# A two-block transformer kernel on one core: paired score adds, a row-wise output projection, a smaller candidate gather, and twelve hidden tiles computed earlier

## The chip, the cores and the metric

The kernel runs on one core of one Trainium2 chip. The metric is the device time of one execution in microseconds. Before the change three runs took 3618.88, 3621.45 and 3625.93 us; their median is 3621.45 us. The profile used here comes from one further execution of 3620.09 us, of which the traced span is 3618.3 us; the 1.8 us outside the span are left as they are.

## The reference, cut to what matters

Two transformer blocks follow one another on 512 tokens of width 1024, in float32. The first block (attention and a mixture of 32 experts) is not touched. The second block is:

```python
def second_block(x, ...):
    h = rmsnorm(x, norm1_g)
    a_val, a_gate, q, k, v, f_logit, g_a, g_b = jnp.split(h @ w_in, idx, axis=-1)
    ya = conformer_conv(a_val, a_gate, conv_w, ...)            # 31 taps, 1024 channels
    c = jnp.cumsum(log_sigmoid(f_logit + fox_bf), axis=1)
    ob = forgetting_attention(q, k, v, c)                      # 16 heads of 64; s = q k / 8 + c_q - c_k, causal
    yb = ob @ w_fox_out
    x = x + (sigmoid(g_a) * ya + sigmoid(g_b) * yb) @ w_out    # the "last projection"
    x = x + peer_ffn(rmsnorm(x, norm2_g), ...)
    return rmsnorm(x, normf_g)

def peer_ffn(h, ...):                                          # 8 heads, 16384 experts
    s1, s2 = ...                                               # two sets of 128 scores per token and head
    v1, i1 = lax.top_k(s1, 16); v2, i2 = lax.top_k(s2, 16)
    cand = v1[..., :, None] + v2[..., None, :]                 # 256 sums, top 16 of them
    sc, pos = lax.top_k(cand, 16)
    experts = i1[pos // 16] * 128 + i2[pos % 16]
    gates = softmax(sc)
    a = gelu(u[experts] . h) * gates                           # u, v: 16384 x 1024
    return sum(a * v[experts])
```

## The kernel before, in words

A float32 product is made of three matmuls on rounded high and low parts (`mm3`: high by high, high by low, low by high). The splits into parts are made on ScalarE (high part, a copy) and VectorE or GpSimd (low part, a subtraction). The instruction order on each engine is the program's order, written by hand; no scheduler moves anything. Engines meet through buffers and semaphores.

The stages that the change touches, in order of time:

*Attention of block 2* (`attend`, called by `block2`, 32 units: 8 head pairs by 4 query blocks of 128 tokens, keys 128 to 512). In step t the loop issues the scores of unit t, its row maximum and exponential (`soft`), the normalisation of unit t-1, the transposes of unit t-2 and the product with the values of unit t-3. Between the steps it issues six taps of the convolution on VectorE (`background`) and one or two pieces of other projection work (`work`). `scores` computes the two heads of a pair, each from 64 partitions, into two PSUM tiles; behind each one stands a bf16 matmul over 96 partitions that adds the decay c_q - c_k, with weights `L` that `make` builds on VectorE, one instruction per head.

*Last projection* (`block2`, lines 1675 to 1692). For each of 8 blocks of 128 output columns, `zT` multiplies a weight block (stationary) with the 512 tokens (moving), so the result comes out transposed. ScalarE copies it out, four TensorE transposes turn it, VectorE adds it to the rows `xt`, and ScalarE makes four sums of squares.

*Routing* (`peer_route`). For each of 8 heads: two projections, scores, the top 16 of both score sets (`top16`), then `choose` (50 candidate sums, top 16 of them), `ranks` (one-hot of 16 positions by 50), `codes` (times the codes, on GpSimd), `gather` (a reduction over 50). VectorE carries most of it.

*Hidden tiles* (`split_u`, `first`, `first_one`). There are 128 tiles of 128 experts; one `first` is 24 matmuls of 384 columns (tokens 0 to 383; the last 128 tokens take the sparse way) and a GELU into an `act` tile. `NPRE` = 34 of them are issued ahead of the last stage: 20 in routing, 10 in the gate stage, 4 at the start of the last stage.

*Gate stage* (`peer_gates`). In 48 steps of 8 tokens, one-hot tiles `o1`, `o2` are built on GpSimd (three instructions a step), VectorE and ScalarE, multiplied on TensorE (`gps`), and written to DRAM. A `first` is put between the steps, with its low-part split on GpSimd.

*Last stage* (`peer`). 128 iterations. While hidden tiles are left, an iteration holds one `first` and one `second` (18 matmuls of 512 columns); afterwards only a `second`. VectorE also works through 256 gathered rows (`row`) for the last 128 tokens, spread over the iterations.

## Time and profile before

| | us |
|---|---|
| median of three runs | 3621.45 |
| profiled execution, whole | 3620.09 |
| its span | 3618.3 |
| TensorE busy | 3469.0 (96%) |
| VectorE busy | 2951.5 (82%) |
| ScalarE busy | 2029.2 (56%) |
| GpSimd busy | 1189.7 (33%) |

A busy TensorE is not by itself a bound, since matmuls are pipelined and overlap in the records; a stage is read by what the next instruction waited for. Up to 1709 us nothing is changed. The stages that follow are told apart by the lines of their first instructions: attention of block 2 from 1718 us, its gates and two projections from 2046 us, the last projection from 2220 us, routing from 2275 us, the gate stage from 2503 us, the last stage from 2652 us, its part without hidden tiles from 3455 us, the final norm from 3604 us.

### The profile page before, as it was taken

How to read it: one execution, taken by the hardware profiler on the slowest of the kernel's cores; microseconds unless marked ns; L12 is line 12 of the kernel's file. 1: busy time of each engine (PE TensorE's matmuls, PEld its weight loads, DVE VectorE, ACT ScalarE, POOL GpSimd, SP SyncE). 2: the span in 40 equal slices, each digit the busy share in tenths (PEclk: the TensorE clock that was granted, in tenths of full speed). 3: DMA queues.
4: the chain of work that ended last, by engine and by line, in shares of the span. 5: the costliest groups of instructions: out<-in, count | busy, mean ns of one | idle time of the engine just before them, and what ended most of it. 6: DMA issues, size and time to landing. Idle time of an engine off the chain costs nothing.

```text
span 3618.3 us, 48096 instructions
## 1 busy us (share of the span) xinstructions
PE 3469.0 (96%) x16965; PEld 2799.1 (77%) x16966; DVE 2951.5 (82%) x4755; ACT 2029.2 (56%) x3225; POOL 1189.7 (33%) x756
## 2 busy tenths in 40 slices
PE   8899879999999999998999999998999999999998
PEld 5665667777777777776777778787888889988976
DVE  5676489999999999997888754799967777777777
ACT  4555468888888888886434353424853333333333
POOL 0567022222222222220000000467954444433333
PEclk9889989999999999999999999999999999999999
DMA  5322579999999999993121222322578888888886
GB/s 201 103 94 97 184 276 373 367 370 373 363 371 364 369 364 374 369 358 102 68 70 59 70 93 87 102 80 88 210 289 300 300 301 297 296 306 292 294 281 225
DMA packets 229994, 866.56 MB, mean 239 GB/s; under 512 B 21890, under 2 KB 73218, under 8 KB 179060
## 3 DMA queue, kind: packets, MB, share of 16 engines
q1 hardware_dynamic: 131680, 641.33, 47.7%
q0 software_dynamic: 47008, 170.87, 14.5%
q10 hardware_dynamic: 51060, 51.23, 4.2%
q8 instruction: 136, 2.23, 0.2%
q14 instruction: 110, 0.90, 0.1%
HBM read 815.05 MB, written 48.30 MB: 239 GB/s over the span
## 4 chain that ended last, share of the span: by engine, by line
PE 43%; DVE 5%; POOL 3%; ACT 1%; issue 0%; DMA 0%; ACTq 0%; DVEq 0%; POOLq 0%
PE out L2056 15%; PE mm L133 4%; PE mm L134 4%; PE mm L135 4%; PE a L135 4%; PE a L134 4%; PE a L133 4%; POOL o L1954 2%; PE sc L992 1%; DVE eq L1843 1%; POOL ul L1731 1%; PE ot L1046 1%; DVE ex L1851 1%; DVE t L1931 1%; PE pt L1031 0%
## 5 line engine op out<-in xcount | busy, mean ns | idle before, releaser
L1123 DVE TENSOR_TENSOR elo<-raw,ehi 128x1024 fp32r<-128x1024 f32 x384 | 460.6, 1250 | 8.5 <-ACT ehi L1121 8.5
L1121 ACT ACTIVATE ehi<-raw 128x1024 fp32r<-128x1024 f32 x384 | 380.0, 1047 | 9.2 <-PE y L1231 9.2
L135 PE MATMUL a<-hT,ul 128*128 128x384 f32 x1024 | 347.6, 339 | 21.3 <-POOL ul L1731 20.7
L133 PE MATMUL a<-hT,uh 128*128 128x384 f32 x1024 | 347.0, 339 | 1.3 <-ACT uh L1730 1.3
L134 PE MATMUL a<-hT,uh 128*128 128x384 f32 x1024 | 345.3, 337 | 0.0
L1231 PE MATMUL u<-ehi,xgTh 128*128 128x512 f32 x1024 | 337.9, 411 | 0.7 <-ACT xgTh L1165 0.7
L1231 PE MATMUL u<-ehi,xgTl 128*128 128x512 f32 x1024 | 322.9, 396 | 0.0
L1231 PE MATMUL u<-elo,xgTh 128*128 128x512 f32 x1024 | 322.3, 396 | 0.0
L2056 PE MATMUL out<-vh,ah 128*128 128x512 f32 x768 | 302.8, 394 | 1.7 <-ACT ah L125 1.7
L2056 PE MATMUL out<-vl,ah 128*128 128x512 f32 x768 | 303.1, 395 | 0.0
L1123 DVE TENSOR_TENSOR elo<-hT,ehi 128x1024 fp32r<-128x1024 f32 x256 | 296.6, 1218 | 0.5 <-ACT ehi L1121 0.5
L2008 ACT ACTIVATE vh<-vr 128x1024 fp32r<-128x1024 f32 x128 | 135.8, 1061 | 281.9 <-issue 187.4
L2021 POOL DMA_INDIRECT gu<-in_peer_u,pidx x128 | 197.7, 1545 | 248.6 <-DVE gu L2030 225.7
L2021 POOL DMA_INDIRECT gu<-in_peer_v,pidx x128 | 182.5, 1426 | 285.6 <-DVE h L2037 260.0
L2009 DVE TENSOR_TENSOR vl<-vr,vh 128x1024 fp32r<-128x1024 f32 x128 | 156.7, 1225 | 142.6 <-ACT vh L2008 140.3
L1190 POOL DMA_INDIRECT x_d<-ysb,row x31 | 72.0, 2324 | 586.5 <-DVE ysb L1284 527.3
L133 PE MATMUL mm<-hT,sh 128*128 128x512 f32 x648 | 262.8, 406 | 0.0
L135 PE MATMUL mm<-hT,sl 128*128 128x512 f32 x648 | 256.5, 396 | 0.1
L1121 ACT ACTIVATE ehi<-hT 128x1024 fp32r<-128x1024 f32 x256 | 249.2, 1047 | 0.0
L2056 PE MATMUL out<-vh,al 128*128 128x512 f32 x768 | 241.3, 395 | 0.0
L134 PE MATMUL mm<-hT,sh 128*128 128x512 f32 x584 | 231.6, 396 | 0.6 <-DVE hT L1415 0.6
L1231 PEld LDWEIGHTS u<-ehi,xgTl 128*128 128x128 f32 x1024 | 192.9, 188 | 47.0 <-DVE xgTl L1166 0.5
(570 smaller groups left out, 8620.9 us busy)
## 6 DMA issues: line engine op xcount, KB each, us to landing
raw<-in_exp_w SPq DMA_DIRECT2D x192, 1024.0 KB, 7.6
hT<-in_exp_w SPq DMA_DIRECT2D x128, 1024.0 KB, 6.9
sraw<-in_w SPq DMA_DIRECT2D x128, 512.0 KB, 3.3
xt<-in_exp_w SPq DMA_DIRECT2D x64, 1024.0 KB, 8.6
ur<-in_peer_ut SPq DMA_DIRECT2D x128, 512.0 KB, 6.0
vr<-in_peer_vt SPq DMA_DIRECT2D x126, 512.0 KB, 5.7
adaw<-in_ada_w SPq DMA_DIRECT2D x96, 256.0 KB, 4.2
G_d<-G ACTq DMA_DIRECT2D x12, 2048.0 KB, 6.7
```

Source lines behind the costliest of these rows:

```text
L133: nc.tensor.matmul(ps, lh, rh, start=start, stop=False)
L134: nc.tensor.matmul(ps, lh, rl, start=False, stop=False)
L135: nc.tensor.matmul(ps, ll, rh, start=False, stop=stop)
L1121: nc.scalar.activation(hi, src, AF.Copy)
L1123: eng.tensor_tensor(lo, src, hi.bitcast(F), op=OP.subtract)
L1190: nc.gpsimd.indirect_dma_start(out=self.x_d, in_=y, in_offset=None, compute_op=OP.add, out_offset=bass.IndirectOffsetOnAxis(ap=self.row[:, ...
L1231: nc.tensor.matmul(dst[n], x, w[:, n * 512:n * 512 + 512], start=ch >= 8 and k == 0 and x is xh and w is hi, stop=k == KC - 1 and w is lo)
L1954: nc.gpsimd.tensor_scalar(o1[:, i], io, e1[:, t + i:t + i + 1], None, op0=OP.is_equal)
L2008: nc.scalar.activation(hi, r, AF.Copy)
L2009: nc.vector.tensor_tensor(lo, r, hi.bitcast(F), op=OP.subtract)
L2021: nc.gpsimd.indirect_dma_start(out=gu[i], out_offset=None, in_=A["peer_u" if i < 128 else "peer_v"], in_offset=bass.IndirectOffsetOnAxis(a ...
L2056: nc.tensor.matmul(out[tb][n], x, w[:, n * 512:n * 512 + 512], start=i == 0 and x is ah and w is hi, stop=i == 127 and x is al)
```

## The change: what it does

Five edits.

1. *Decay adds in pairs.* The two score matmuls of a unit stand next to each other, then the two decay adds. The decay parts are laid out in 64 partitions per head of a pair instead of 96 shared ones, so that `L` is one tile for both heads and one `make` instruction replaces two.
2. *Last projection by rows.* The tokens are stationary and the weights move in 512 columns; the weights are laid out anew on the host. Four PSUM tiles (token blocks) per half of the columns take 24 matmuls each. There are no copies and no transposes; VectorE adds each tile to `xt`, ScalarE makes one sum of squares for each.
3. *Gather by parts.* 54 candidates instead of 50, in such an order that the first eight of the sixteen winners lie among the first 20. `ranks`, `codes` and `gather` work on 8 by 20 and 8 by 54 elements instead of 16 by 50, with two instructions for each one of before.
4. *Twelve more hidden tiles ahead.* `NPRE` goes from 34 to 46: three more behind the last head of routing, nine more in the gate stage. In the gate stage every second low-part split is issued on VectorE. The additional `act` tiles lie in the buffers of `xt` (and two constants), so the rows `xt` are written to DRAM at the start of routing (four transfers of 512 KB on ScalarE's queue, ahead of the norm gain) and read back in iteration 104 of the last stage.
5. *Order in the last stage.* The product with the gates, then some gathered rows, then the splits, then the rest of the rows, instead of all rows at the end of an iteration; the rows are spread over 128 iterations by the new `NPRE`.

```diff
@@ attend
+            extra = u.get("add")
             for i in range(2):
                 ps = psp.tile([128, 512], F, name=f"sc{i}", bufs=scb)
-                extra = u.get("add")
                 nc.tensor.matmul(ps[:, :n], u["q"][i], u["k"][i], start=True, stop=extra is None)
-                if extra is not None:
-                    nc.tensor.matmul(ps[:, :n], *extra(i), start=False, stop=True)
                 s["ps"].append(ps)
+            if extra is not None:
+                for i in range(2):
+                    nc.tensor.matmul(s["ps"][i][:, :n], *extra(i), start=False, stop=True)
...
@@ block2
-            L[j] = at.tile([96, 2, S], BF, name="L", bufs=2)
-            for i in range(2):
-                h = 2 * j + i
-                nc.vector.tensor_scalar(L[j][:, i], cp, fm[:96, 2 + 2 * h:3 + 2 * h], fm[:96, 3 + 2 * h:4 + 2 * h],
-                                        op0=OP.mult, op1=OP.add)
+            L[j] = at.tile([128, S], BF, name="L", bufs=2)
+            nc.vector.tensor_scalar(L[j], cp, fm[:, 4 + 2 * j:5 + 2 * j], fm[:, 5 + 2 * j:6 + 2 * j],
+                                    op0=OP.mult, op1=OP.add)
...
-                    add=lambda i, j=j, qs=qs, n=n: (L[j][:, i, qs], R[:, :n]),
+                    add=lambda i, j=j, qs=qs, n=n: (L[j][half(i), qs], R[half(i), :n]),
...
-        for j in range(8):
-            ps = out_T(v, sgb)
-            t = pl.tile([128, S], F, name="yT", bufs=2)
-            nc.scalar.activation(t, ps, AF.Copy)
...
+        self.close(psl, psm)
+        pso = self.pool("pso2", bufs=2, space=PSUM)
+        for n in range(2):
+            ps = [pso.tile([128, 512], F, name=f"o{tb}") for tb in range(TB)]
+
+            def part(k, tb, w):
+                ts = slice(tb * 128, tb * 128 + 128)
+                hi, lo = (x.rearrange("p k n -> p (k n)")[:, k % 2 * 512:][:, :512] for x in w)
+                for i, (x, y) in enumerate(((v[k], hi), (v[k], lo), (sgb[k], hi))):
+                    nc.tensor.matmul(ps[tb], x[:, ts], y, start=k + i == 0, stop=k == KC - 1 and i == 2)
+
+            for c in range(4):
+                w = next(self.w2)
+                for k, tb in ([(k, tb) for tb in range(TB) for k in (6, 7)] if c == 3 else
+                              [(k, tb) for k in (2 * c, 2 * c + 1) for tb in range(TB)]):
+                    part(k, tb, w)
+            for tb in range(TB):
+                x = self.xt[tb][:, 512 * n:512 * n + 512]
+                nc.vector.tensor_tensor(x, x, ps[tb], op=OP.add)
+                sq = pl.tile([128, 512], BF, name="sq2", bufs=2)
+                nc.scalar.activation(sq, x, AF.Square, accum_out=self.ss8[:, tb, n:n + 1])
...
-    NPRE, NX = 34, 6
+    NPRE, NX, NH = 46, 6, 12
...
@@ peer_route
+        for tb in range(TB):
+            nc.scalar.dma_start(self.x1_d[tb * 128:tb * 128 + 128, :], self.xt[tb])
         g = nt.tile([128, D], F, name="ngain")
...
-            st[h] = pq.tile([128, TB, 16, 50], F, name="eq"), pos, code
+            st[h] = pq.tile([128, TB, 8, 20 + 54], F, name="eq"), pos, code
...
+        parts = (slice(0, 20), slice(0, 8), 20), (slice(20, 74), slice(8, 16), 54)
...
-            for i in range((1, 2, 2, 2, 2, 2, 2, 3)[h]):
+            for i in range((1, 2, 2, 2, 2, 2, 2, 6)[h]):
...
@@ peer_gates
-                self.split_u(self.done + 1, nc.gpsimd)
+                self.split_u(self.done + 1, (nc.gpsimd, nc.vector)[self.done % 2])
                 self.first()
...
@@ peer
+            a = gated(i + 1) if i < 127 else None
+            rows(i + 0.5)
             self.split_u(self.done + 1, nc.vector)
...
             split(i + 1)
-            nxt = weigh(i + 1) if i < 127 else None
+            nxt = parts(a) if i < 127 else None
             self.first()
             second(i, cur)
...
+            if i == 104:
+                self.x_tiles()
+                for tb in range(TB):
+                    nc.scalar.dma_start(self.xt[tb], self.x1_d[tb * 128:tb * 128 + 128, :])
+            rows(i + 1)
```

Where the order moves. First, TensorE in the attention of block 2, the unit of head pair 4 with 512 keys, before:

```order
L135 MATMUL mm<-hT,sl 128x512
L992 MATMUL sc_16949<-k_16080,q_16072 128x512
L994 LDWEIGHTS L
L994 MATMUL sc_16949<-R,L 128x512
L992 MATMUL sc_16952<-k_16080,q_16072 128x512
L994 LDWEIGHTS L
L994 MATMUL sc_16952<-R,L 128x512
L1031 MATMUL pt_16969<-ident,ap_16797 128x128 x2
```

and after:

```order
L135 MATMUL mm<-hT,sl 128x512
L992 MATMUL sc_16944<-k_16080,q_16072 128x512
L992 MATMUL sc_16946<-k_16080,q_16072 128x512
L996 LDWEIGHTS L
L996 MATMUL sc_16944<-R,L 128x512
L996 LDWEIGHTS L
L996 MATMUL sc_16946<-R,L 128x512
L1032 MATMUL pt_16964<-ident,ap_16792 128x128 x2
```

The second head's scores moved ahead of the first head's decay add, so that two matmuls on 64 partitions each follow one another twice.

Second, ScalarE at the start of routing, with the projection copy `q` and the first hidden tile, before:

```order
L1414 ACTIVATE hT<-tr,colv 128x512 x5
L1730 ACTIVATE uh<-ur 128x1024
L1771 DMA ngain<-in_norm_g 128x1024
L1782 DMA keys<-in_peer_k 128x256 x2
L1796 ACTIVATE q_20826<-mm 128x512
L202 ACTIVATE sh<-sraw 128x1024
```

and after (`x_d<-xt` is the transfer of the rows to DRAM):

```order
L1415 ACTIVATE hT<-tr,colv 128x512 x5
L1732 ACTIVATE uh<-ur 128x1024
L1781 DMA x_d<-xt 128x1024 x4
L1783 DMA ngain<-in_norm_g 128x1024
L1794 DMA keys<-in_peer_k 128x256 x2
L1808 ACTIVATE q_20736<-mm 128x512
L202 ACTIVATE sh<-sraw 128x1024
```

Four transfers now stand ahead of the gain that `h4` on VectorE needs; the copy `q` of the first projection is behind `h4` in its buffer.

Third, VectorE at the start of the gate stage, from the last copy of routing (`pg`) over the first two builds of one-hot tiles (`w`, `o`, `o`), before:

```order
L1918 COPY pg_20672<-g 128x128
L1955 TENSOR_TENSOR w_22933<-io_20674,eT 128x512
L1959 TENSOR_TENSOR o_22931<-io_20674,eT 128x640
L1962 TENSOR_SCALAR o_22932<-io_20674,eT 128x128 x4
L1955 TENSOR_TENSOR w_22950<-io_20674,eT 128x512
L1959 TENSOR_TENSOR o_22948<-io_20674,eT 128x640
L1962 TENSOR_SCALAR o_22949<-io_20674,eT 128x128 x4
L1955 TENSOR_TENSOR w_23011<-io_20674,eT 128x512
```

and after:

```order
L1947 COPY pg_20578<-g 128x128
L1984 TENSOR_TENSOR w_22977<-io_20580,eT 128x512
L1988 TENSOR_TENSOR o_22975<-io_20580,eT 128x640
L1991 TENSOR_SCALAR o_22976<-io_20580,eT 128x128 x4
L1984 TENSOR_TENSOR w_22994<-io_20580,eT 128x512
L1988 TENSOR_TENSOR o_22992<-io_20580,eT 128x640
L1991 TENSOR_SCALAR o_22993<-io_20580,eT 128x128 x4
L1733 TENSOR_TENSOR ul<-ur,uh 128x1024
L1984 TENSOR_TENSOR w_23055<-io_20580,eT 128x512
```

The low-part split `ul` of a hidden tile now stands on VectorE between two builds; the next one follows six builds later, and the splits between them stay on GpSimd.

## Rows read from the trace of the kernel before

**Rows 1.** Windows A:B: length, busy us of PE, PEld, DVE, ACT, POOL; clock, DMA share, GB/s

```profile
1718.00:2046.00 328.00, 327.92 (x1607) 234.42 (x1606) 279.48 (x508) 130.82 (x278) 10.43 (x11) 1.00 0.19 64
2275.40:2503.50 228.10, 203.81 (x1034) 182.47 (x1034) 212.19 (x974) 67.04 (x90) 133.68 (x44) 0.94 0.25 85
2503.50:2652.00 148.50, 137.48 (x1010) 131.68 (x1011) 143.51 (x286) 117.57 (x305) 144.85 (x153) 0.99 0.48 192
2652.00:3455.00 803.00, 801.00 (x4028) 722.50 (x4027) 587.30 (x731) 292.37 (x385) 334.33 (x231) 1.00 0.86 300
3455.00:3604.00 149.00, 147.29 (x629) 117.59 (x628) 120.22 (x141) 57.78 (x75) 51.98 (x32) 1.00 0.77 262
```

**Rows 2.** Timeline of PE, one head pair of block 2: start us, us, instruction

```profile
1883.62 0.48 PE L992 MATMUL sc<-k,q 64*128 64x128 f32 x2
1884.68 0.82 PE L1031 MATMUL pt<-ident,ap 128*128 128x128 f32 x6
...
1916.06 1.12 PE L992 MATMUL sc<-k,q 64*128 64x512 f32 x2
1917.11 0.39 PE L994 MATMUL sc<-R,L 96*128 96x512 bf16 x1
...
1918.71 0.60 PE L1031 MATMUL pt<-ident,ap 128*128 128x128 f32 x4
...
1925.40 0.49 PE L992 MATMUL sc<-k,q 64*128 64x128 f32 x2
```

**Rows 3.** Timeline of PE, a unit of block 1's attention, which has no decay add

```profile
377.96 1.13 PE L992 MATMUL sc<-km,qm 64*128 64x512 f32 x4
```

**Rows 4.** Waits of DVE, 1718 to 2046 (total, times, longest); instruction of `make`

```profile
DVE zc L1508 <- PE mm L135: 16.2, 8, 2.3
DVE aw L1006 <- PE sc L994: 3.6, 4, 2.7
...
L1559 DVE TENSOR_SCALAR L<-cpart,colv x16: 402/403/406, 1717.9 to 1982.4; 96x512 bf16<-96x512 bf16 x16
```

**Rows 5.** Timeline of PE and DVE, first and last of the last projection [idle before]

```profile
2220.12 0.40 PE L133 MATMUL mm<-v,sh 128*128 128x512 f32 x1
...
2270.82 0.66 PE L1683 MATMUL lsum<-ident,yT 128*128 128x128 f32 x4 [2.79 <-ACT yT L1678]
...
2273.76 0.19 DVE L1766 TENSOR_REDUCE ss<-ss 128x4 f32<-128x32 f32 x1 [1.36 <-ACT sq L1689]
```

**Rows 6.** Timeline of DVE and ACT, start of routing

```profile
2290.26 1.49 DVE L1772 SCALAR_TENSOR_TENSOR h<-xt,rs,ngain 128x1024 f32<-128x1024 f32 x1 [2.24 <-DMA ngain<-in_norm_g]
...
2292.71 0.60 ACT L1796 ACTIVATE q<-mm 128x512 f32<-128x512 f32 x1 [4.53 <-DVE h L1772]
```

**Rows 7.** Groups of DVE in routing, six heads: busy us, mean ns, idle before

```profile
L1843 DVE TENSOR_TENSOR eq<-io,pos 128x3200 f32<-128x3200 f32 x6 | 20.9, 3492 | 0.2
L1851 DVE TENSOR_REDUCE ex<-eq 128x64 f32<-128x3200 f32 x6 | 20.8, 3464 | 0.0
```

**Rows 8.** Timeline of PE, end of routing

```profile
2471.82 0.69 PE L135 MATMUL a<-hT,ul 128*128 128x384 f32 x1 [9.98 <-POOL ul L1731]
...
2503.50 1.90 PE L1976 MATMUL gps<-o,o 128*128 128x128 f32 x8 [2.38 <-ACT o L1958]
```

**Rows 9.** Groups in the gate stage; below them a piece of the chain

```profile
L1954 POOL TENSOR_SCALAR o<-io,eT 128x128 f32<-128x128 f32 x142 | 120.1, 866 | 0.0
L1976 PE MATMUL gps<-o,o 128*128 128x128 f32 x752 | 95.5, 282 | 13.4 <-POOL o L1954 10.6 <-ACT o L1958 2.4
...
L1731 POOL TENSOR_TENSOR ul<-ur,uh 128x1024 fp32r<-128x1024 f32 x10 | 26.0, 2598 | 2.3 <-ACT uh L1730 2.2
...
2646.61 5.37 PE gps L1976 x48
```

**Rows 10.** Chain of waits, two iterations of the last stage: start us, us

```profile
2679.76 4.20 PE out L2056 x18
2688.14 4.20 PE out L2056 x18
```

More of the change, by code (lines that the diff above doesn't have):

```diff
@@ L2047, in weigh, with rows @@
             return ah, al
+        def rows(i):
+            nonlocal done
+            k = 128 - self.NPRE
+            while done < min(256, 256 * (min(i, k) + 0.42 * max(0, i - k)) / (k + 0.42 * (127 - k))):
+                row(done)
+                done += 1
+                if done == 253:
+                    g = dn.tile([128, D], F, name="gu", bufs=NG)
+                    nc.sync.dma_start(g, bcast_rows(A["normf_g_2"], D))
+                    gain.append(g)
         def second(i, a):
@@ L2193, in layout @@
         put(n, col(f(n + "_2")))
[L2194 to L2199 removed]
+    par, part, side, p = (a.reshape(128) for a in np.indices((2, 4, 2, 8)))
+    heads, real = 2 * p + par, part < 3
+    put("fox_bf", f("fox_bf_2").reshape(16)[heads].reshape(128, 1))
+    fm = np.zeros((128, 20), np.float32)
+    fm[:, 0], fm[:, 1] = -1.0 * (real & (side == 0)), real & (side == 1)
+    fm[:, 2], fm[:, 3] = -1.0 * (part >= 1), -1.0 * (part >= 2)
+    for j in range(8):
+        fm[:, 4 + 2 * j], fm[:, 5 + 2 * j] = (real & (side == i) & (p == j) for i in (1, 0))
     put("foxmask", fm)
```

132 lines of the change are left out of this document (65 added, 67 removed).

## Prediction

> **What bounds the kernel now.** I read the windows by stage first, then in each changed stage the waits of the engine that ends last, and the timeline where two engines meet. The reader is to see four different limits. In the attention of block 2 TensorE has work all the time (327.9 of 328 us), and VectorE is close behind with 279 us [rows 1]; it waits for TensorE only 16.2 and 3.6 us in all [rows 4]. In routing VectorE works 212 of 228 us while TensorE runs dry in places, ten microseconds at once near the end [rows 1, 8]. In the gate stage GpSimd is busy 144.9 of 148.5 us and never waits between its one-hot builds, while TensorE waits for it [rows 1, 9]. In the last stage TensorE has no gap, and an iteration is a hidden tile of 8.38 - 4.20 = 4.18 us and a `second` of 4.20 us [rows 10]. So work that leaves TensorE counts in full in attention and in the last stage, and work put on TensorE is cheap only where it waits now.
>
> All sums go against the profiled execution, 3620.1 us, which lies 1.4 us under the median of the three runs and inside their spread.
>
> **Decay adds in pairs.** A unit with 512 keys takes 1918.71 - 1916.06 = 2.65 us of TensorE, of which one head's scores take 1917.11 - 1916.06 = 1.05; one with 128 keys takes 1.06 us [rows 2]. The two sizes between lie on a line, so 32 units take 32 x 1.86 = 59 us. Without an add between them, the scores of two heads take 1.13 us together in block 1, as long as one head's here [rows 3]: they overlap, being on different halves of the partitions. The pair saves 1.05 of 2.65, 40%, or 24 us. The bf16 adds come on 64 partitions each now, for which there is no row. If they overlap as well it is half, 30 us; if not, 24 us. VectorE's work stays, except for 8 of 16 `make` instructions of 0.40 us [rows 4]. It can become faster only by the time it waits for TensorE: 16.2 + 3.6 + 3.2 = 23 us, less than TensorE saves. So VectorE becomes the bound here. An engine that works in order does not give back every wait, so I take -20 us, with -14 to -23 for the range.
>
> The Trainium skill says the same on its page "TensorEngine Tiling (Array Packing)", section "PSUM Bottleneck": tiling speeds up TensorE, not the evacuation of PSUM, which can become the limit. By TensorE alone this part would be -27 us and the total 3562 us; by the rule it is VectorE's wait time, as above. No run here shows that limit yet.
>
> **Last projection.** It is 8 x 24 matmuls of 512 columns before and 2 x 96 after, so the matmul time stays: 192 x 4.20/18 = 44.8 us [rows 10], from 2220.12 to 2264.9 [rows 5]. Now TensorE ends at 2270.82 - 2.79 = 2268.0; the transposes between are gone, -3.1 us. From there to the sum of the squares it takes 2273.76 - 2268.0 = 5.7 us (copy, turn, two adds, four squares) [rows 5]; afterwards one add and one square of 512 columns, about 0.75 + 0.6 + 0.2 us from the 1024-column pass and the 512-column copy [rows 6]. That is -4 us. The new PSUM tiles take all banks and may wait for the old ones' last reader, +1 us. I take -6 us (-4 to -7).
>
> **Routing.** One head has 3.49 us of `ranks` and 3.46 us of `gather` [rows 7]; 8 x (20 + 54) elements for 16 x 50 are 0.74 of that, so -0.9 us each. Two instructions for one and 54 candidates for 50 cost some 0.3 us a head (no row; between 0 and 0.6). Seven heads lie ahead of the point where TensorE waits for the split behind `codes` [rows 8]: 7 x 1.5 = -10.5 us (-8 to -12).
>
> At its start four transfers of 512 KB go ahead of the norm gain on ScalarE's queue. VectorE waits 2.24 us for the gain already, and ScalarE's copy of the first projection waits 4.53 us behind `h4` [rows 6]. At the 300 GB/s of the last stage [rows 1] 2.1 MB are 7 us. TensorE's first hidden tile, 4.18 us, stands between projection and scores and covers a part. I take +4 us (0 to +9); without that cover it would be the 9.
>
> At its end there are eight hidden tiles instead of five between the last scores and the gate stage. That stretch takes 2503.50 - 2471.82 = 31.7 us [rows 8], in which TensorE has 20.9 us of tiles; eight are 33.4 us, so it becomes TensorE's. The exponential of the gates stands behind three more GELUs on ScalarE, and `codes` of the last head behind three more splits on GpSimd, so VectorE gets both later. Three tiles cost 12.5 us if nothing hides them; I take +9.5 us (+6 to +12.5).
>
> **Gate stage.** TensorE's own work is 384 products of 5.37/24 = 0.224 us [rows 9], 86 us, and 10 x 4.18 = 42 us of hidden tiles: 128 of 148.5 us. With 19 tiles it is 86 + 79 = 165 us. GpSimd, the bound now with 120 + 26 us [rows 9], loses one split of ten. VectorE gets ten splits, which have no row in this stage: between 1.5 us (the 1024-column pass [rows 6]) and GpSimd's 2.6 us each [rows 9], so 15 to 26 us on top of 143.5 [rows 1]. So TensorE becomes the bound, with VectorE just under it. In order, the GELU holds ScalarE until a tile ends, and the split holds its engine until ScalarE's copy comes, which delays the next build; I put 5 us on that. Together +22 us (+17, TensorE without a gap, to +32).
>
> **Last stage.** Twelve iterations lose their hidden tile: 12 x 4.18 = -50 us. VectorE has 256 gathered rows over fewer long iterations, by the loop's formula 2.54 for 2.38 in each, and was busy 587 of 803 us [rows 1]; that is covered. In the short iterations it is busy 120 of 149 us [rows 1], and the rows rise from 1.00 to 1.07 an iteration: covered, thinly. Reading `xt` back, 2.1 MB where the DMA share is 0.77, may hold up a weight tile: 0 to +4 us; I take 0, since the loads run two tiles ahead.
>
> **Sum.** -20 - 6 - 10.5 + 4 + 9.5 + 22 - 50 = -51 us, so 3569 us. The move of the twelve tiles brings 50 us and gives back 31.
>
> **Rivals.**
> *More is hidden.* The gate stage costs only TensorE's 17 us, the end of routing 6, its start nothing, and attention gives VectorE's whole 23 us: 3620 - 66 = 3554 us. For it speaks that TensorE runs without a gap wherever it is fed now; against it the in-order waits above. Chance 0.16.
>
> *The pairs do not overlap in block 2*, for example because the bf16 adds or the banks' readers keep them apart: attention gives nothing, -31 us, 3589 us. Against it stands what block 1 shows [rows 3]. Chance 0.08.
>
> *The gate stage hides nothing.* VectorE, busy 97% of the stage now, becomes its bound with the splits at their upper price and the blocked builds: nine tiles at full price, +37 us, 3584 us. Chance 0.10.
>
> *Slower: the gathers bound the long iterations.* Each moves two tiles and 2.54 gathered rows of 512 KB and 0.2 MB of gates, 2.6 MB where it was 2.5. The DMA share is 0.86 at 300 GB/s [rows 1], so it should come to 0.89. If the gathers clog the queues, the 81 long iterations stretch; from 9.0 us each (286 GB/s) the 51 us are gone, and at 9.2 us it is 3635 us. It would need the engines to do less than they do now. Chance 0.03.
>
> *The change does not do what it says*: two of the above at once, with no measurable difference. Chance 0.03.
>
> **How the numbers follow.** The forecast has 0.60, around 3569 us. The range from 3552 to 3588 us takes in the bounds of the terms, half of the first rival, the third one and part of the second; outside lie about 0.18. Faster by over 0.2% (about 7 us, what a measurement of this kernel can tell from no change) are the forecast and the first three rivals, 0.94; the same 0.03; slower 0.03.
>
> **What would show it.** In the profile after: score matmuls in groups of four with one duration, the 41.8 us between head pairs [rows 2] down to about 39, and VectorE's wait for `zc` near zero; no transposes in the last projection, and 1.5 to 2 us from its last matmul to the sum of squares; `ranks` and `gather` at 2.6 to 2.7 us in two pieces; the first use of the gain some 7 us later than its issue was; the gate stage 165 to 180 us long, with TensorE busy and GpSimd waiting; 81 iterations of 8.38 us and 47 of 4.20. The prediction is wrong in its main part if attention keeps 41.8 us a pair, if the gate stage grows by more than 32 us, or if a long iteration is over 8.5 us.

## The result and the profile after

Four runs of the changed kernel took 3576.52 to 3579.89 us, median 3578.07 us; four runs of the kernel before beside them 3614.23 to 3625.93, median 3620.16 us. The ratio is 0.9886, with a 95% interval of 0.9872 to 0.9900. The change brings 42 us; the forecast was 51 us, and the time lies inside the range.

The profiled execution took 3579.89 us (span 3578.1), 40.2 us less than the profiled one of before. This is where the 40.2 us are, stage by stage; both columns are starts read from the two traces:

| stretch | before, us | after, us | measured | forecast |
|---|---|---|---|---|
| up to the first score of block 2 (code not changed) | 1720.6 | 1717.8 | -2.8 | 0 |
| first score to first matmul of the last projection | 499.5 | 475.9 | -23.5 | -20 |
| last projection, to the first `nrow` | 55.3 | 47.6 | -7.7 | -6 |
| routing, to the first `gps` | 228.1 | 229.8 | +1.7 | +3 |
| gate stage, first to last `gps` | 148.2 | 182.2 | +34.0 | +22 |
| last `gps` to first `second` | 27.9 | 27.3 | -0.6 | 0 |
| first to last matmul of `second` | 924.4 | 884.0 | -40.4 | -50 |
| tail | 14.3 | 13.4 | -0.9 | 0 |

Two rows miss: the gate stage by 12 us and the last stage by 10 us. The first row is no effect of the change: in the thirteen profiled executions of the changed kernel and its variants that stretch, with the same code, ended between 1717.4 and 1723.8 us. So single profiles are compared here by stretches, not by their ends. How far a stretch varies by itself is seen on the gate stage: in the seven profiles that run it as the change has it, it takes 181.1 to 182.2 us.

**Attention.** The timeline of TensorE (start us, us, instruction), the units with 512 and 128 keys, answers to [rows 2]:

```profile
1899.22 1.13 PE L992 MATMUL sc<-k,q 64*128 64x512 f32 x4
1900.18 0.38 PE L996 MATMUL sc<-R,L 64*128 64x512 bf16 x2
1907.25 0.49 PE L992 MATMUL sc<-k,q 64*128 64x128 f32 x4
1907.58 0.22 PE L996 MATMUL sc<-R,L 64*128 64x128 bf16 x2
...
1946.04 0.49 PE L992 MATMUL sc<-k,q 64*128 64x128 f32 x4
```

Both heads' scores take 1.13 us, exactly block 1's pair [rows 3], and both bf16 adds 0.38 us, what one took before. A unit of 512 keys is down from 2.65 to 1.34 us (1900.18 + 0.38 - 1899.22), and the cycle of a head pair from 41.8 to 1946.04 - 1907.25 = 38.8 us. The waits of VectorE between the first and the last score (total, times, longest), beside [rows 4]:

```profile
DVE k L1564 <- ACT q L1563: 9.2, 7, 1.3
DVE sl L203 <- ACT sh L202: 8.0, 2, 6.3
DVE aw L1007 <- PE sc L996: 2.9, 1, 2.9
DVE zc L1508 <- PE mm L135: 2.6, 7, 0.9
```

The wait for `zc` has gone from 16.2 to 2.6 us. What is left are mainly waits for ScalarE.

**Last projection.** TensorE and VectorE, first matmul, last matmul and sum of squares, beside [rows 5]:

```profile
2193.76 0.47 PE L1683 MATMUL o<-sh,v 128*128 128x512 f32 x1 [0.87 <-DVE v L1665]
...
2237.76 0.40 PE L1683 MATMUL o<-sh,sgb 128*128 128x512 f32 x1
...
2239.74 0.16 DVE L1775 TENSOR_REDUCE ss<-ss 128x4 f32<-128x8 f32 x1 [0.71 <-ACT sq L1694]
```

TensorE runs 2237.76 + 0.40 - 2193.76 = 44.4 us without a gap worth naming, and the squares come 2239.74 - 2238.16 = 1.6 us behind it.

**Start of routing**, beside [rows 6] (the number in brackets is the idle time ahead):

```profile
2256.07 1.23 ACTq L1783 DMA_DIRECT2D ngain<-in_norm_g  x1
...
2263.06 1.28 DVE L1784 SCALAR_TENSOR_TENSOR h<-xt,rs,ngain 128x1024 f32<-128x1024 f32 x1 [8.56 <-DMA ngain<-in_norm_g]
...
2265.29 0.60 ACT L1808 ACTIVATE q<-mm 128x512 f32<-128x512 f32 x1 [10.63 <-PE a L135]
...
2268.35 0.89 DVE L1955 MAX8 v<-s 128x8 f32<-128x128 f32 x4 [4.00 <-PE s L1820]
...
2430.17 0.69 PE L135 MATMUL a<-hT,ul 128*128 128x384 f32 x1 [8.23 <-POOL ul L1733]
```

The gain lands 7.0 us after its issue, behind four writes of 512 KB on the same queue; `h4` waits 8.56 us for 2.24, and ScalarE's `q` 10.63 for 4.53. The first top-16 step starts 27.0 us after `nrow` (2241.37) where it was 24.1: +2.9 us. From there to the point where TensorE waits for the split behind `codes` (the last line, beside [rows 8]) it is 161.8 us where it was 172.3, -10.5 us, and from that point to the first `gps` 41.0 us where it was 31.7, +9.35 us.

**Gate and last stage.** Windows over routing, the gate stage (length, busy us of PE, PEld, DVE, ACT, POOL, granted clock, DMA share, GB/s), beside the second and third of [rows 1]:

```profile
2241.40:2471.20 229.80, 211.70 (x1106) 189.91 (x1106) 204.32 (x1001) 71.00 (x96) 141.04 (x55) 0.97 0.31 101
2471.20:2653.70 182.50, 175.32 (x1226) 170.35 (x1227) 149.30 (x296) 131.28 (x324) 143.73 (x152) 0.98 0.48 182
```

VectorE's busy time in routing falls from 212.2 to 204.3 us. In the gate stage TensorE works 175 of 182.5 us, at a mean granted clock of 0.98. GpSimd is busy 143.7 us; these are the longest waits of the stage, of all engines (total, times, longest):

```profile
POOL ul L1733 <- ACT uh L1732: 33.2, 9, 5.7
DVE ul L1733 <- ACT uh L1732: 30.1, 10, 4.4
ACT xt L1762 <- PE a L135: 19.4, 10, 2.5
ACT act L1762 <- PE a L135: 16.6, 8, 3.2
PEld gps L2005 <- POOL o L1983: 11.9, 25, 1.3
ACT G L2007 <- PE gps L2005: 6.4, 8, 1.6
PE gps L2005 <- POOL o L1983: 6.3, 11, 1.1
```

GpSimd's 143.7 + 33.2 us are 177 of 182.5. It waits for ScalarE's copy `uh`, before it may make the low part of a split; before the change that wait was 2.2 us [rows 9]. VectorE waits for the same copy, and its 149.3 + 30.1 us fill the stage as well, so these sums do not tell which engine holds it. What TensorE waits for does: its longest waits, and those of its weight loads, are for GpSimd's one-hot tiles `o` (6.3 and 11.9 us), and none in the list is for VectorE.

In the last stage the long iterations take 8.38 us as before [rows 10]. 80 x 8.38 + 48 x 4.20 = 872.0 us (the trace has 80 long iterations between the first and the last `second`, not the 81 of the prediction) would lead from the first `second` to the end; it took 884.0. The missing 12 us are in the short iterations (before: 92 x 8.38 + 36 x 4.20 = 922.2 of 924.4, so 2.2 us). A piece of the chain of waits there (start us, us):

```profile
3454.18 8.63 DMA vr<-in_peer_vt
...
3462.92 1.07 ACT vh L2037
3464.01 1.24 DVE vl L2038
3465.26 7.76 DMA vr<-in_peer_vt
...
3475.48 6.92 DMA vr<-in_peer_vt
```

It is a circle: the load of a tile is issued when the split of an earlier one sets its buffer free, takes 6.9 to 8.6 us, and the split of the new tile sets the next one going. Two buffers go round in that circle, so a turn of 10 us gives two tiles, where TensorE wants two in 8.4 us. ScalarE waits 86.0 us for `vr` in this stretch (26 times) against 5.2 us (4 times) before. Most of that TensorE does not notice: in the short iterations it stands still for 6.6 us in all. How a late load reaches it (start us, us, instruction, idle time ahead):

```profile
3535.99 1.06 ACT L2037 ACTIVATE vh<-vr 128x1024 fp32r<-128x1024 f32 x1 [6.20 <-DMA vr<-in_peer_vt]
3536.96 0.51 ACT L125 ACTIVATE ah<-act 128x384 fp32r<-128x384 f32 x1
...
3537.51 0.49 PE L2101 MATMUL out<-vh,ah 128*128 128x512 f32 x1 [2.20 <-ACT ah L125]
```

TensorE waits for `ah`, the high part of the gated hidden tile, and `ah` stands behind `vh` in ScalarE's order, though its input was ready at 3531.6. TensorE's listed waits in the short iterations are 3.9 us for `ah` and 2.4 us for `vl`. Whether `ah` ahead of `vh` would make the late loads harmless was not tried. Then there is a second loss (windows of 4 us, columns as above):

```profile
3532.00:3536.00 4.00, 3.31 (x15) 2.31 (x13) 0.77 (x1) 0.01 (x1) 0.94 (x1) 1.00 1.03 403
3536.00:3540.00 4.00, 2.13 (x6) 1.51 (x7) 2.92 (x4) 2.93 (x4) 0.00 (x0) 0.89 0.59 198
3540.00:3544.00 4.00, 4.00 (x14) 3.14 (x13) 3.71 (x5) 0.00 (x1) 0.00 (x0) 0.68 0.60 206
3544.00:3548.00 4.00, 4.00 (x19) 3.21 (x18) 2.68 (x4) 1.47 (x2) 0.00 (x0) 1.00 0.46 163
```

TensorE is busy 2.13 of 4 us, and in the next 4 us the granted clock is 0.68 on average, that is, partly at the lower level of 1.2 GHz: 14 matmuls for 19. The two windows below 1.00 cost 0.11 x 4 + 0.32 x 4 = 1.7 us. So 6.6 us of idle time and 1.7 us of clock are found of the 12; the remaining 4 us or so are not seen in the records, which show TensorE as busy there.

### The profile page after: what moved, and what is told of

It is laid out like the page before. It is cut to its first block, busy times and chain, and to the rows that moved or that the text cites. A ratio compares the mean times of both kernels' runs of the same rounds, so it can differ in the third digit from the quotient of the medians.

```text
span 3578.1 us, 48012 instructions
## 1 busy us (share of the span) xinstructions
PE 3431.6 (96%) x16933; PEld 2775.1 (78%) x16934; DVE 2918.9 (82%) x4762; ACT 2002.3 (56%) x3169; POOL 1151.7 (32%) x766
## 4 chain that ended last, share of the span: by engine, by line
PE 35%; DVE 9%; DMA 3%; ACT 3%; POOL 2%; issue 1%; ACTq 0%; DVEq 0%; SPq 0%; POOLq 0%
PE out L2101 12%; PE a L135 4%; PE a L133 4%; PE a L134 4%; PE mm L133 3%; PE mm L135 3%; PE mm L134 3%; DMA vr<-in_peer_vt 2%; DVE conv L1514 2%; PE o L1683 1%; POOL o L1983 1%; POOL ul L1733 1%; PE gps L2005 1%; ACT o L1987 1%; ACT G L2007 1%
## 5 line engine op out<-in xcount | busy, mean ns | idle before, releaser
L2050 POOL DMA_INDIRECT gu<-in_peer_v,pidx x128 | 163.6, 1278 | 292.3 <-DVE h L2066 274.2
L2050 POOL DMA_INDIRECT gu<-in_peer_u,pidx x128 | 169.5, 1324 | 243.2 <-DVE gu L2059 229.4
```

The lines of the kernel that those rows point to most:

```text
L2050: nc.gpsimd.indirect_dma_start(out=gu[i], out_offset=None, in_=A["peer_u" if i < 128 else "peer_v"], in_offset=bass.IndirectOffsetOnAxis(a ...
```

## The experiments

Each starts from the changed kernel. Times are medians with the ratio to the kernel before on the same chip; where there is one run only, stretches of its profile are compared.

**The order in the gate stage: the split issued earlier**

```diff
+            tile = self.done < n and t8 >= (self.done - at) * gap
+            if tile:
+                self.split_u(self.done + 1, (nc.gpsimd, nc.vector)[self.done % 2])
             if t8 < 47:
                 nxt = build(8 * t8 + 8)
...
-            if self.done < n and t8 >= (self.done - at) * gap:
-                self.split_u(self.done + 1, (nc.gpsimd, nc.vector)[self.done % 2])
+            if tile:
                 self.first()
```

> The changed kernel, with one edit: in the gate stage the split of a hidden tile is issued ahead of the next one-hot build and of the two copies of G, not behind them. Theory (the order holds the stage): GpSimd and VectorE wait 33 and 30 us for ScalarE's uh, which stands behind the copies of G and so behind TensorE. One step earlier that wait mostly goes, GpSimd builds on, and the stage falls from 182 us to about 170 (to 173 at least), so -8 to -14 us in all. Rival (TensorE is the bound: it is busy 175 of the 182.5 us): at most its 7 us of gaps can go, so 0 to -5 us and TensorE's busy time stays at 175.

Measured: 3569.61 us, 0.9857 (0.9840 to 0.9873). The stage takes 174.3 us, -7.9. Window of the stage, and GpSimd's wait in it:

```profile
2473.50:2648.30 174.80, 170.22 (x1227) 166.96 (x1228) 150.35 (x296) 131.15 (x324) 144.15 (x152) 1.00 0.50 190
```

```profile
POOL ul L1733 <- ACT uh L1732: 27.4, 9, 3.4
```

The theory holds, at the lower end: the order is worth 7 to 8 us (the run "The reading back spread" below has the same order in this stage and takes 175.3). The rival's limit of 5 us is passed, and TensorE's busy time falls by 5 us though its work is the same. Some 3 of these 5 us are the granted clock, 0.98 on average in the changed kernel and 1.00 here; the rest may be matmuls stretched by late operands, which no run isolates. GpSimd still waits 27 us and VectorE 22 us for `uh`: one step is not far enough ahead.

**The order in the gate stage: all splits on GpSimd**

```diff
-                self.split_u(self.done + 1, (nc.gpsimd, nc.vector)[self.done % 2])
+                self.split_u(self.done + 1, nc.gpsimd)
```

> The changed kernel, with all splits of the gate stage on GpSimd, as before the change, and none on VectorE. Theory (the order holds the stage, not an engine's work): GpSimd gets nine more splits of 2.5 us, 22 us on 144 busy of 182.5, and still has room; the stage changes by less than 5 us either way. Rival (GpSimd's own work bounds it): 144 + 22 = 166 us plus the 38 us that it waits for uh, so +15 us or more.

Measured: 3574.01 us, 0.9867 (0.9851 to 0.9884); stage 176.2 us, -6.0. Window and wait of the same kind:

```profile
2478.50:2655.20 176.70, 171.47 (x1227) 168.44 (x1228) 158.43 (x286) 130.79 (x324) 164.25 (x162) 0.99 0.47 186
```

```profile
POOL ul L1733 <- ACT uh L1732: 11.2, 15, 1.6
```

Both expectations miss. GpSimd does 20 us more work and the stage is shorter, so its own work was not what the stage waited for. But it has no room left either: 164.3 + 11.2 = 175.5 of 176.7 us. It arrives later at each split and waits less for `uh`. Putting ten splits on VectorE, which the change does, cost 6 us in this order instead of helping.

**The price of a tile in the gate stage**

```diff
-        n = self.NPRE - 4
+        n = self.NPRE - 4 - 6
...
+        for i in range(6):
+            self.split_u(self.done + 1, nc.vector)
+            self.first()
         for i in range(4):
```

> The changed kernel with 13 hidden tiles in the gate stage for 19; the other six run one after the other behind it, with nothing beside them (25 us if TensorE never waits, more if the weight transfers bound them). By the two profiles a tile costs 34/9 = 3.8 us in the gate stage, of its 4.18. If that price is the same for each, the six give back 23 us for 25 or more: +2 to +6 us. Rival (only the last tiles are dear, since the first nine find GpSimd's slack): the stage falls by more than 25 us and the kernel becomes faster by up to 5 us. If the six were half hidden, as the prediction had it (22 us for nine), it is +10 us.

Measured: 3585.40 us, 0.9896 (0.9880 to 0.9913). The stage takes 159.4 us, and from its end to the first `second` it is 55.1 us for 27.3. So six tiles free 22.8 us, 3.8 each, and cost 27.8 us in the open, 4.6 each: +5 us by stretches, as the constant price says. The price of 3.8 us per tile, of 4.18, is the same from 13 to 19 tiles as from 10 to 19. As ordered, the gate stage hides next to nothing.

**Four buffers in the short iterations**

```diff
-                raw[i] = dn.tile([128, D], F, name="vr", bufs=2)
+                if i >= 84 and i % 4 > 1:
+                    raw[i] = self.du.tile([128, KC, 128], F, name="ur", bufs=2).rearrange("p k n -> p (k n)")
+                else:
+                    raw[i] = dn.tile([128, D], F, name="vr", bufs=2)
...
-                load(i + 2)
+                if i < 82:
+                    load(i + 2)
...
+                if i >= 84:
+                    load(i + 4)
```

The splits 82 and 83 issue the loads 84, 86, 87 and 85.

> The changed kernel, with four buffers for the rows of peer_vt in the short iterations of the last stage (the two of ur, free by then, and the two of vr) and loads four tiles ahead for two. Theory (late transfers: the two-tile lead of 8.4 us is too short for single transfers while others burst): ScalarE's waits of 86 us for vr nearly go and the last stage ends 8 to 12 us earlier. Rival (bandwidth: 305 GB/s are wanted and the engines are busy 0.86 to 0.9 of the time): the lead is used up and the waits come later, 0 to -4 us.

Measured: 3573.50 us, 0.9871 (0.9855 to 0.9888), four runs between 3569.98 and 3576.68. The stretch of `second` takes 872.7 us, 0.7 more than the sum of its iterations. ScalarE's wait for `vr` in it:

```profile
  DMA vr<-in_peer_vt: 4.3, 1
```

The theory of late transfers holds: the loads land no sooner (after a median of 7.0 us for those into the buffers of `vr` and 5.2 for those into the buffers of `ur`; 6.0 in the changed kernel, 4.6 before), and TensorE no longer notices. The rival, bandwidth, is out in this profile: 299 GB/s were moved between 3360 and 3550 us with TensorE standing still for 0.7 us. The median fell by 4.6 us only, and not by 11: two of the four runs took 3570 us, the profiled one among them, and two 3577. In the profiled one VectorE waits 3.5 us, once, for the gates `gt`; the next run shows what a longer wait of this kind costs, but of the two longer runs here there is no trace.

**The four together** (early split, all splits on GpSimd, four buffers, and this)

```diff
         for h in range(2):
             load_keys(h)
+        for tb in range(TB):
+            nc.scalar.dma_start(self.x1_d[tb * 128:tb * 128 + 128, :], self.xt[tb])
```

with the same two lines taken out ahead of `ngain`.

> The changed kernel with four edits: the split of a hidden tile ahead of the next build and the copies of G (as in the first run), all splits of the gate stage on GpSimd (as in the second), four buffers for the rows of peer_vt in the short iterations (as in the fourth), and on ScalarE's queue the norm gain and the first two keys ahead of the four writes of x_d. If the gains stand apart: -8 (gate stage) - 4 to -6 (no split on VectorE) - 11 (last stage, by its profile) - 3 (start of routing) = -26 to -28 us, so 3550 to 3552 us. Rival: the first two gains are one and the same wait (that for uh), so -8 and not -13; then 3555 to 3558 us, with a gate stage of 172 to 175 us. A third: with the split early GpSimd becomes the bound of the gate stage (144 + 22 us and its waits), 176 us or more.

Measured: 3567.81 us, 0.9857 (0.9840 to 0.9873): the gains do not add up, and the third expectation comes nearest. Start of routing: `h4` waits 2.4 us for 8.6, and the first `gps` starts 750.5 us after the first score for 753.4, -2.9. Gate stage: 181.2 us, no gain, as the third expectation says: GpSimd is busy 163.4 us and waits 13.9 for `uh` and 2.2 for VectorE, 179.5 of 181.7. Each of the two edits helps alone; together they do not. With the same work on GpSimd the stage took 176.7 us in the old order, so that work is not the whole reason; why this order makes the stage 5 us longer is not shown. Last stage: 878.3 us in spite of the four buffers. A wait of VectorE and the windows around it:

```profile
DVE act L2089 <- DMA gt<-G_d: 6.5, 1, 6.5
```

```profile
3480.00:3484.00 4.00, 3.89 (x17) 2.80 (x15) 0.00 (x0) 0.83 (x1) 0.00 (x0) 1.00 0.45 172
3484.00:3488.00 4.00, 0.73 (x2) 0.41 (x3) 3.17 (x4) 1.58 (x2) 1.14 (x1) 0.83 0.25 67
3488.00:3492.00 4.00, 4.00 (x10) 3.13 (x11) 4.00 (x6) 0.52 (x1) 1.54 (x2) 0.50 1.08 356
3492.00:3496.00 4.00, 4.00 (x15) 3.17 (x15) 1.37 (x3) 1.35 (x2) 1.01 (x1) 0.82 1.01 368
```

The gates `gt` were issued on ScalarE's queue at 3463.1, behind the four reads of `xt` at 3450.7 to 3452.1, and its reader could start at 3484.8. TensorE stood for some 3.4 us, and the granted clock went to 0.50 for the next 4 us: ten matmuls where there are nineteen. So the reading back has a price of its own, through the queue, once the loads of `vr` no longer hide it.

**Without the reading back**

```diff
-                    nc.scalar.dma_start(self.xt[tb], self.x1_d[tb * 128:tb * 128 + 128, :])
+                    nc.vector.memset(self.xt[tb], 0.0)
```

> The changed kernel without the reading back of xt at iteration 104; xt is set to zero there instead, so the residual is left out of the result. The last stage takes 884.0 us from the first product of second to the last, of which 80 x 8.38 + 48 x 4.20 = 872.0 are accounted for; with four buffers it took 872.7. If the 2.1 MB cause the waits for vr: 872 to 875 us. If the row order and the thin lead cause them and the read only adds its own share (the waits began at 3447 us, before it is issued at 3456): 878 to 882 us.

Measured: 882.2 us for the stretch of `second`, ScalarE waits 61.9 us for `vr` (20 times). So those waits do not need the 2.1 MB. The run is not quite clean: the zeroing is four VectorE instructions of 0.91 us each in the same iteration, and a stop of TensorE of 1.2 us follows them. The stretch differs from run to run: with the last stage as changed it took 884.0, 880.9, 879.1, 883.0, 875.6 and 878.1 us in six profiles, and 882.2 lies among them.

**No decay adds**

```diff
-            extra = u.get("add")
+            extra = None
```

> The changed kernel without the decay products in the scores of block 2 (that term is left out of the result). From the first score to the first product of the last projection it takes 475.9 us. If VectorE bounds attention, as the prediction has it, TensorE's 32 x 2 x about 0.15 to 0.25 us or some 12 us less change nothing: 473 to 476 us, with VectorE's busy share up and TensorE waiting more. If TensorE still bounds it (it is busy 299 of 303 us): 462 to 467 us.

Measured, from the first score to the last: 297.2 us for 298.1. The windows, of this kernel and of the changed one:

```profile
1719.50:2016.70 297.20, 290.44 (x1519) 216.85 (x1518) 269.94 (x491) 127.69 (x278) 10.46 (x11) 1.00 0.20 67
```

```profile
1717.80:2015.90 298.10, 294.23 (x1583) 219.35 (x1582) 270.38 (x492) 127.90 (x278) 10.44 (x11) 1.00 0.21 67
```

TensorE's busy time falls by 3.8 us (the expectation had put 12; the adds overlap with each other and with the scores) and the stretch by 0.9. So TensorE's time no longer counts in full, though it is still busy 290 of 297 us: that fits VectorE setting most of the pace, with its 270 us of work and 23 us of waits, but no run took work from VectorE to test it.

**Adds per head again**

```diff
             for i in range(2):
                 nc.tensor.matmul(ps[:, :n], u["q"][i], u["k"][i], start=True, stop=extra is None)
+                if extra is not None:
+                    nc.tensor.matmul(ps[:, :n], *extra(i), start=False, stop=True)
```

> The changed kernel with the order of before in the scores (scores of a head, its decay add, then the next head), but with the adds still on 64 partitions. If it is the grouping in pairs that pays, the cycle of two heads goes back towards 41.8 us, and the stretch from the first score to the last projection from 475.9 to 490 to 499 us. If the halves alone are enough (the second head's scores beside the first head's add, on other partitions), it stays within 5 us of 475.9.

Measured: 298.1 us from the first score to the last, the same to 0.1 us. The unit with 512 keys:

```profile
1902.27 1.13 PE L992 MATMUL sc<-k,q 64*128 64x512 f32 x4
1903.23 0.39 PE L995 MATMUL sc<-R,L 64*128 64x512 bf16 x2
```

Once the adds stand on 64 partitions, the grouping is worth nothing: in the order of before, the step from 96 to 64 partitions alone gives the whole gain (2.65 to 1.35 us for this unit). An add over 96 partitions touches the partitions of both heads, and there the second head's scores did not start beside it; on 64 partitions they do. Grouping with adds over 96 partitions was not run, so what it would have brought by itself is not shown.

**The reading back spread** (with the early split, in turn on GpSimd and VectorE, four buffers, and the gain ahead)

```diff
-            if i == 104:
+            if i == 92:
                 self.x_tiles()
-                for tb in range(TB):
-                    nc.scalar.dma_start(self.xt[tb], self.x1_d[tb * 128:tb * 128 + 128, :])
+            if i in (92, 100, 108, 116):
+                tb = (i - 92) // 8
+                nc.scalar.dma_start(self.xt[tb], self.x1_d[tb * 128:tb * 128 + 128, :])
```

> The changed kernel with the early split (taken in turn by GpSimd and VectorE, as in the first run), four buffers for the rows of peer_vt, the norm gain and keys ahead of the writes of x_d, and xt read back one tile at a time at iterations 92, 100, 108 and 116 instead of four at 104, so that gt never stands behind four of them on ScalarE's queue. If the parts stand apart: gate stage 174 us (-8), first to last product of second 872 to 874 us (-10 to -12), gain -3: 3554 to 3558 us. Rival: the last stage stays at 878 us or more because it is short of bandwidth whatever the order of the transfers is; then 3562 us or more.

Measured: 3561.47 us, 0.9835 (0.9819 to 0.9852). `second` takes 872.3 us, its iterations' sum to 0.3 us, at 338 GB/s in one stretch of 50 us (3350 to 3400); gate stage 175.3 us; first score to first `gps` 750.3 us. The parts stand apart. The profiled execution took 3557.5 us, the shortest of the four; the median is 3.5 us above the expectation.

**All splits of the gate stage on VectorE**, else as the last

```diff
-                self.split_u(self.done + 1, (nc.gpsimd, nc.vector)[self.done % 2])
+                self.split_u(self.done + 1, nc.vector)
```

> The run before, with all splits of the gate stage on VectorE. VectorE: 138 + 19 x 1.23 = 161 us of work, GpSimd 120. If GpSimd's work and its waits set the stage (it took 181 us with all early splits there), it falls to 168 to 172 us, TensorE's own 166 being the floor; the whole 2 to 6 us under the run before. If VectorE's waits for uh hold its part of the next build and so ScalarE's o, the stage is 175 to 182 us, the whole the same or up to 8 us slower.

Measured: 3557.75 us, 0.9822 (0.9806 to 0.9839), four runs between 3557.16 and 3558.50. Gate stage 173.8 us. Window of it, and waits:

```profile
2470.70:2645.00 174.30, 170.26 (x1227) 167.41 (x1228) 141.67 (x305) 130.74 (x325) 127.84 (x143) 1.00 0.50 191
```

```profile
POOL o L1983 <- PE gps L2008: 39.1, 22, 2.9
ACT o L1987 <- DVE w L1984: 38.6, 23, 2.1
...
PE gps L2008 <- ACT o L1987: 3.6, 5, 2.4
PE gps L2008 <- DVE o L1988: 2.6, 7, 0.5
```

Now GpSimd waits for TensorE, 39 us, and no longer the other way. TensorE works 170 of 174 us at full clock, so at most 4 us of gaps are left there; VectorE's 141.7 us of work and 30.6 us of waits for `uh` fill the stage too, and which of the two would have to give next is not shown. Both expectations missed by some microseconds. This version beats both kernels: it is 65 us under the kernel before on its chip, where the changed kernel is 42 us under the one measured beside it. Against the run before this one the stage is only 1.6 us shorter, and that run starts the stage at a lower granted clock (0.63 in its first 4 us, 1.00 here), so the stage does not tell what moving the splits is worth.

What a split on GpSimd does to VectorE shows in the trace of the changed kernel, and no expectation had it:

```profile
2508.16 2.67 POOL L1733 TENSOR_TENSOR ul<-ur,uh 128x1024 fp32r<-128x1024 f32 x1 [5.73 <-ACT uh L1732]
2508.51 3.32 DVE L1991 TENSOR_SCALAR o<-io,eT 128x128 f32<-128x128 f32 x4
```

Four such one-hot instructions take 1.1 us elsewhere. Beside each of the 9 splits on GpSimd in this stage one of them takes 2.4 to 2.6 us, where the median of all is 0.34, and it ends within 0.1 us of the split. One VectorE instruction is held in the same way beside each of the 10 splits before the change and beside 18 of the 19 with all splits on GpSimd; with all splits on VectorE the longest takes 0.47 us. So a split on GpSimd costs VectorE some 2.1 us in which it is counted as busy, more than the 1.23 us that VectorE takes to make the split itself. With the early order the stage takes 181.2, 175.3 and 173.8 us for 19, 9 and no splits on GpSimd; how much of that is GpSimd's time and how much VectorE's was not separated.

**Fewer rows in the short iterations**

```diff
-... 0.42 * max(0, i - k)) / (k + 0.42 * (127 - k))
+... 0.36 * max(0, i - k)) / (k + 0.36 * (127 - k))
```

> The changed kernel with the weight of a short iteration 0.36 for 0.42 in the row schedule: 0.94 gathered rows in a short iteration for 1.07, and 2.6 in a long one for 2.54. Two buffers for the rows of peer_vt as in the change. If the 7% more gathers are what makes the loads of vr late (1.28 MB in 4.20 us, 305 GB/s): the last stage falls from 876 to 884 us to 872 to 875, and ScalarE's waits for vr from 62 to 86 us to 20 or less. If not: 876 to 884 us as in the other runs.

Measured: 878.5 us; ScalarE waits 40.0 us for `vr` (11 times, 19 to 26 times in the runs above), and the loads land after a median of 4.8 us for 5.3 to 6.0. The number of gathers may play a part (878.5 us lies among the other runs, but the waits are the shortest of them), and not all of it: 6.5 us are still missing, 2.9 of them in the 50 us around the reading back, where TensorE is busy 47.1.

**All rows at the end of an iteration**

```diff
             a = gated(i + 1) if i < 127 else None
-            rows(i + 0.5)
```

> The changed kernel with all rows of an iteration at its end, as before the change, and none between the gate product and the split; still 1.07 rows in a short iteration. If the order is what makes the loads late (the load is issued behind the split, and the split now stands behind a row on VectorE): waits for vr of 20 us or less and 872 to 875 us in the last stage. If the number of rows does it: 876 to 884 us as in the other runs.

Measured: 878.3 us, 62.9 us of waits for `vr`. The place of the rows makes no difference that stands out of the spread of the runs.

So in the last stage neither the reading back, nor the number of rows, nor their place is the cause alone; each run without one of them lies within the 875.6 to 884.0 us of the others. What all share is the circle of two buffers, and with four it is gone. How much of the longer landing time each transfer brings was not settled. The reading back removed together with fewer rows was not tried.

## Why the prediction was right, and where it was not

*Attention (-20, measured -23.5).* Right, and by its mechanism: the scores and adds of two heads overlap, TensorE saves about half of a unit, the cycle falls to 38.8 us, and TensorE is no longer the limit in full, which moves most likely to VectorE. What the prediction had wrong is the condition: it let the scores overlap because no add stands between them, but with an add on 64 partitions between them they overlap just as well. From the first score to the last it is 25.1 us. VectorE's listed waits fall from 40.7 to 22.7 us (18.0) and its busy time from 276.7 to 270.4 us (6.3, of which 2.3 are `make`; three taps of the convolution, 2.1 us, have only moved out of this window), together 24.3. The bound of 23 us had left out the wait for ScalarE's `sh`, which fell by 3.7 us as well.

Here the Trainium skill's page "TensorEngine Tiling (Array Packing)", section "PSUM Bottleneck", had been cited, by which tiling speeds up TensorE but not PSUM evacuation. The trace agrees in part. Another engine does set the limit: the last 3.8 us that were taken from TensorE brought 0.9. But it is not evacuation that fills it: 166.8 of VectorE's 270.4 us in this stretch are the taps of the convolution.

*Last projection (-6, measured -7.7).* Right in both parts: 44.4 us of matmuls (forecast 44.8), 1.6 us to the squares (forecast 1.5 to 2). The microsecond set aside for PSUM banks was not needed.

*Routing (+3, measured +1.7).* Right in each of its three parts. At its start +2.9 for a forecast of +4, and undone by moving the four writes behind the keys; -10.5 over seven heads, as forecast; +9.35 at its end for +9.5. `ranks` are 1.95 us for the large piece (1728 elements) and 0.83 for the small one (640), 2.8 in all, a little over the 2.6 to 2.7 of the forecast. At its end the exponential does come late: VectorE waits 5.3 us for it.

*Gate stage (+22, bound +32, measured +34.0).* The step that failed is "TensorE becomes the bound, with VectorE just under it", with 5 us for the order. By the prediction's own sign, a gate stage that grows by more than 32 us, its main part is wrong here. TensorE still waited for GpSimd's tiles, now because of its place in the order and not of its work: GpSimd stood 33.2 us in waits for `uh`. The split stands in its order between two builds and waits for `uh`, which ScalarE makes only behind two copies of G and the GELU, both of which wait for TensorE; so builds come late, and TensorE's matmuls with them. The size splits in two. With the order mended and the splits on VectorE the stage takes 173.8 us, with TensorE busy 98% of it: so 26 of the 34 us are what nine tiles cost where TensorE has hardly a gap. The forecast had 17 for that, since it counted the 768 `gps` matmuls at the pace of one unbroken run, 86 us, where even the best run shows 93.7 us busy for them, and its own [rows 9] showed 95.5. The other 8 us are the order, some 3 of them through the granted clock, where 5 had been put. The rival "the gate stage hides nothing" (+37) was nearer to the measured time, but its reason was not the measured one: VectorE was busy 149 of 182 us, its ten splits took 1.23 us each where 1.5 to 2.6 had been put, and TensorE waited for GpSimd. That a split on GpSimd holds VectorE, 10 times 2.1 us of the 143.5 in [rows 1], was in no term.

*Last stage (-50, measured -40.4).* The long iterations are right to the digit, and so is the DMA share there (0.89). The term that failed is that of reading `xt` back, "0 to +4 us; I take 0, since the loads run two tiles ahead", and with it "covered, thinly" for the rows: 12 us are missing where 2 were before. The price was looked for in bytes, and the cover in the lead of two tiles. But the lead is what gave way: a load of 4.6 us fits into two tiles of 4.20, one of 7 to 8.6 us with the split behind it does not; the run with four buffers, where the loss is gone, shows it. What makes the loads land later than before the change stays open. The reading back was the wrong suspect for these waits; it has a price of its own (6.5 us of a wait for `gt`), which shows only with four buffers.

*The sum.* -51 forecast, -40.2 in the profile: gate stage +12, last stage +10, against -3.5 in attention, -1.7 in the projection, -1.3 in routing, -1.5 at the joints and the tail, and -2.8 from stages that the change does not touch. The misses of the large terms add to 22 us; the small ones all went the other way. With the two large misses alone the time would have been about 3591 us, outside the range, so that the range held is in part luck: 2.8 us of the rest come from code that the change does not touch.

## What to carry to other kernels

When work is put into another stage's gaps, add up for each engine not its work alone but its work and the waits that its place in the order gives it. Where several engines fill the stage in that way, as here, the sums do not name the bound, not even TensorE's "busy" 96%: look at what TensorE waited for, and move one instruction in the order to test it. Look also for single instructions that take many times their usual time: here they were VectorE's, held by GpSimd, and were counted as busy. A load with a lead of two tiles is covered only while landing time plus the step that frees the buffer stay below two tiles of work; where a phase has buffers to spare, give them to the loads. Two edits that each help alone can gain nothing together, so the combination has to be run.

## What the runs showed of the hardware that was not expected

- A short stop of TensorE can cost more than its length. After 2.13 busy of 4 us the granted clock was 0.68 in the next 4 us; after 0.73 busy of 4 us it was 0.50 (1.2 GHz) and then 0.82, with 10 and 15 matmuls in 4 us for 19.
- A bf16 matmul of 64 partitions overlaps with a float32 one on the other 64 in either order: 1.34 us for scores and adds of two heads grouped, 1.35 not grouped.
- A load of 512 KB landed 3.3 to 3.6 us after its issue with nothing ahead of it on its queue, and 7.0 us behind four writes of 512 KB; the reader of one of 768 KB behind four reads started 21.7 us after its issue (3463.1 to 3484.8).
- VectorE and GpSimd are not independent: while GpSimd made a low-part split (two float32 inputs, 2.4 to 3.6 us), a VectorE one-hot instruction of 0.34 us took 2.4 to 2.6 us and ended with it, beside each of the 9 splits on GpSimd in the changed kernel's gate stage.
